# Norm steps that run as fill, queued behind the weight splits in a down projection

## The chip, the cores and the metric

The kernel runs on one core of a Trainium2 chip, in one launch. The metric is the device time of one execution in microseconds; the median of the runs counts. A core has TensorE (PE, matrix products), VectorE (DVE), ScalarE (ACT), GpSimd (POOL) and SyncE (SP). Each engine takes its instructions in a fixed order, and an instruction that waits holds what stands behind it on its engine. SP, POOL and ACT also issue DMAs from their queues.

## The reference

Two layers of a diffusion backbone over 1024 latent tokens and 256 context tokens, 1024 channels wide. What matters here is the end of layer 0, and the first norm of layer 1:

```python
def swiglu(u, w_gate, w_up, w_down):
    return (jax.nn.silu(u @ w_gate) * (u @ w_up)) @ w_down

def rms_norm(x, g):
    y = x32 * lax.rsqrt(jnp.mean(x32 * x32, axis=-1, keepdims=True) + RMS_EPS)
    return (y * g.astype(jnp.float32)).astype(x.dtype)
...
        h_lat = h_lat + g2 * swiglu(modulate(rms_norm(h_lat, norm2_g[i]), sh2, sc2), ...)
        if not last:
            h_ctx = h_ctx + cg1 * y_ctx
            h_ctx = h_ctx + cg2 * swiglu(modulate(rms_norm(h_ctx, norm2_g[i]), csh2, csc2), ...)
# next layer:
        u_lat = modulate(rms_norm(h_lat, norm1_g[i]), sh1, sc1)
```

## The kernel before, in words

Channels lie on the 128 partitions, eight blocks deep; tokens lie along the row. They come in pieces: latent half 0 and latent half 1 (512 tokens each, `pc` 0 and 1) and the context (256 tokens, `pc` 2).

Every product is exact to nearly float32 by a split: an operand x becomes `hi`, a rounded copy, and `lo = x - hi`, and the product is the sum of three, hi·hi, hi·lo and lo·hi. `split` makes them: a cast on ACT (L287), then a subtraction on DVE (L289). It notes both instructions in `self.last_hi` and `self.last_lo`. In the context part the weight's halves are called `wh` and `wl`.

`down` (from L1424) is the last product of the feed-forward part. For the latent tokens it runs seven passes of 11 operand pairs each, a fast scheme of seven products in place of eight; each operand (1024 wide) is loaded by SP, split and used by 12 matmuls of 512 columns (L1445), into four accumulators. After a pass, `evict` (L1466) adds the accumulators to the residual on DVE, and `square` makes a square on ACT (L475) and adds it up on DVE (L480). In layer 0 the context part follows: a loop over 22 blocks `kb`. Each loads a weight of 128x1024 (`in_down`, 512 KB), splits it, and runs 24 matmuls of 256 columns (L1557). The staging tile of the weight is a `ws` (two buffers) for two of three blocks, and an `s` of the pool of twenty large tiles for each third (kb 2, 5, 8, 11 and so on); `wh` and `wl` have two buffers each. The context's hidden tile of a block (128x256) is loaded by POOL into one of 35 smaller tiles and split too.

The norm of layer 1 runs as fill in between: `after(pc)`, here `after2` (L1998), is a generator of six steps. The first two compute the scale of each token (`rms_begin`, `rms_end`), and each of the other four norms two channel blocks with `norm_block`: for a block one L522 on DVE (times scale), one L524 on ACT (rounded copy) and one L525 on DVE (the rest). The last reader of a residual tile frees its small buffer. The function `hook(i)` takes the next step; it is called at the start of each of the 11 operand pairs of a latent pass and of each `kb` of the context loop. Half 0's norm begins in the seventh latent pass, half 1's in the context loop. Steps are taken at i = 3 and 6, and in layer 0 at every i > 7.

The order on each engine is not written by hand. A scheduler makes it when the program is built, from the order of the program text, from dependencies and free buffers, and from its own estimate of when each instruction can run. `self.follow(ins)` gives it an edge: what is recorded inside the `with` stands behind `ins` on that instruction's engine. Other places use it already; `evict` stands behind `last_hi` and `last_lo`:

```python
with self.follow(self.last_hi if p < 6 else None), self.follow(self.last_lo if p < 6 else None):
    evict(acc, r, j, q, final)
```

Of the kernel before, what the change touches and what calls it, by code (L numbers as in the profile page):

```python
# [200 lines left out]
class Builder:  # L201
# [1222 lines left out]
    def down(self, l, bops, sops, hidc, hs, h, todo, after, keep):  # L1424
# [57 lines left out]
        done = iter(())  # L1482

        def hook(i):
            if i in (3, 6) or i > 7 and l == 0:
                next(done, None)

        def fetch(p, i):
            ak, bk = seq[p][:2]
# [6 lines left out]
        for p, (ak, bk, r, pc, final) in enumerate(seq):  # L1496
            acc = sets[p % 2]
            late = []
            for i in range(n2):
                hook(i)  # L1500
                if p == 0 and i == 6:
                    load_h(range(4), 1)
                if p == 1 and i in (1, 4, 7):
                    load_h(*((range(4), 0), (range(4, 8), 0), (range(4, 8), 1))[i // 3])
                ops = ready.pop(0) if ready else fetch(p, i)
                if p == 5 and i == n2 - 1:
                    mark = self.last_ld, self.last_hi, self.last_lo
                if p == 6 and i >= n2 - (4 if l else 3):
                    late.append((i, ops))
                else:  # L1510
                    with self.follow(end):
                        for j in range(4):
                            m = prods(acc, ops, j, 0, 512, p in (0, 1, 3) and i == 0, i == n2 - 1)
                    end = m
                if p < 5 and i % 2 or p == 5 and i < 2:
                    next(todo, None)
# [14 lines left out]
            if p == 5:  # L1531
                done = after(0)
        if l == 0:
            for _ in done:
                pass
            done = after(1)
            acc = [self.PP() for _ in range(4)]
            for kb in range(NFB):
                hook(kb)
                if kb in (4, 8, 12, 16):  # L1540
                    load_h((kb // 2 - 2, kb // 2 - 1), 2)
                t = self.S2(F32R)
                f = t[:, 256:].bitcast(F32)
                with self.follow(self.last_ldr):
                    self.ldr(f, hidc[kb // 2][:, kb % 2])
                self.split(f, t[:, :256], t[:, 256:])
                f = self.pw.tile([P, 1024], F32, tag="ws", name=self.nm("ws")) if kb % 3 < 2 else self.S4()
                wh, wl = self.pair1()
                with self.follow(mark[0]), self.follow(mark[1]), self.follow(mark[2]):
                    self.ld(f.rearrange("p (r k) -> p r k", r=2), w[kb].rearrange("r p k -> p r k"))  # L1550
                    self.split(f, wh, wl)
                for nb in range(KB):

                    o = acc[nb // 2][:, nb % 2 * 256:nb % 2 * 256 + 256]
                    with self.follow(end):
                        for k, (x, c) in enumerate(((wh, 0), (wh, 256), (wl, 0))):
                            m = nc.tensor.matmul(o, x[:, nb * P:(nb + 1) * P], t[:, c:c + 256],  # L1557
                                                 start=kb == 0 and k == 0 and nb % 2 == 0,
                                                 stop=kb == NFB - 1 and k == 2, skip_group_check=True)
                    end = m.ins  # L1560
# [640 lines left out]
```

## Time and profile before

| what | value |
|---|---|
| median of 3 runs | 3024.45 us (3024.08 to 3025.89) |
| profiled execution | 3021.79 us, its span 3020.0 us |
| PE busy | 2894.4 us (96%) |
| PE weight loads (PEld) busy | 2414.6 us (80%) |
| DVE busy | 2079.7 us (69%) |
| ACT busy | 1363.0 us (45%) |
| POOL busy | 478.9 us (16%) |
| DMA | 558.26 MB, mean 185 GB/s |

The profile is of one execution, and its times count from the start of the span. A row of the timeline gives start, duration, engine, line of the kernel, operation, the tiles written and read with their shapes, how many instructions were merged into the row, and in brackets how long the engine had been idle before it and what ended that. SPq is the queue on which SP issues DMAs. Adjacent rows of one engine overlap a little, since the end of one instruction runs beside the start of the next.

### The profile page before, as it was taken

Reading aid. Unit: us, or ns where it says so; the run is one execution under the profiler, and the core shown is the slowest. Engines: PE = TensorE matmul, PEld = TensorE weight load, DVE = VectorE, ACT = ScalarE, POOL = GpSimd, SP = SyncE. Lnnn points to the kernel's source line nnn. Section 1 sums busy time; section 2 is a strip of 40 time slices with the busy share of each in tenths; the row PEclk is TensorE's granted clock in tenths of the full one; section 3 lists DMA queues with packets and bytes.
Section 4 is the critical chain, followed back from the end, with each engine's and each line's share of the span. In section 5 each row is a group of like instructions: output and inputs, shape, how many; then the busy total and the mean of one; then the engine's idle time right before and its main releaser. Section 6 shows DMA issues by size and latency. Waiting matters only on the chain. (4 is left out here: it accounts for less than half of the span.)

```text
span 3020.0 us, 45776 instructions
## 1 busy us (share of the span) xinstructions
PE 2894.4 (96%) x16320; PEld 2414.6 (80%) x16320; DVE 2079.7 (69%) x3988; ACT 1363.0 (45%) x2549; POOL 478.9 (16%) x785
## 2 busy tenths in 40 slices
PE   7899999999999999999999999999899999999997
PEld 2678888888899788788888888878777788888886
DVE  5677786675677777876777437777677977665454
ACT  3453325453455333333445337777675533333442
POOL 1112013452100111112020000110111022112000
PEclk9899999999999999999999999999999999999998
DMA  8764545456555554659884344444555266435663
GB/s 279 247 222 168 178 146 172 122 181 230 189 183 196 174 185 170 213 186 324 318 291 155 126 129 118 129 139 124 177 184 203 89 235 216 175 113 184 212 194 119
DMA packets 263486, 558.26 MB, mean 185 GB/s; under 512 B 33878, under 2 KB 85784, under 8 KB 263258
## 3 DMA queue, kind: packets, MB, share of 16 engines
q1 hardware_dynamic: 205050, 372.84, 37.8%
q0 software_dynamic: 55904, 178.30, 16.5%
q10 hardware_dynamic: 2304, 4.20, 0.4%
q8 instruction: 128, 2.10, 0.3%
q14 instruction: 100, 0.82, 0.1%
HBM read 418.63 MB, written 119.80 MB: 178 GB/s over the span
## 5 line engine op out<-in xcount | busy, mean ns | idle before, releaser
L1274 PE MATMUL ps<-s,s 128*128 128x512 f32 x2028 | 505.9, 391 | 12.8 <-ACT g L1279 4.6
L1274 PEld LDWEIGHTS ps<-s,s 128*128 128x128 f32 x2028 | 380.9, 188 | 97.2 <-ACT g L1279 7.1
L283 PE MATMUL ps<-s,wh 128*128 128x256 f32 (+1 forms) x1768 | 393.4, 328 | 2.3 <-DVE s L720 1.2
L283 PEld LDWEIGHTS ps<-s,wh 128*128 128x128 f32 x1768 | 292.7, 189 | 38.1 <-ACT wh L287 2.5
L283 PE MATMUL pq<-s,wh 128*128 128x512 f32 (+1 forms) x984 | 299.4, 383 | 0.6 <-DVE s L1658 0.6
L287 ACT CAST wh<-ws 128x1024 fp32r<-128x1024 f32 (+1 forms) x139 | 142.4, 1024 | 334.7 <-PE ps L283 158.4
L1445 PE MATMUL ps<-s,s 128*128 128x512 f32 (+1 forms) x1000 | 258.4, 383 | 4.5 <-DVE s L289 4.4
L289 DVE TENSOR_TENSOR wl<-ws,wh 128x1024 fp32r<-128x1024 f32 (+1 forms) x139 | 165.3, 1190 | 136.0 <-ACT wh L287 134.2
L283 PE MATMUL ps<-s,wl 128*128 128x256 f32 (+1 forms) x884 | 255.8, 326 | 1.2 <-DVE wl L289 1.2
L287 ACT CAST s<-s 128x1024 fp32r<-128x1024 f32 (+2 forms) x184 | 168.2, 940 | 187.9 <-DMA s<-d 169.6
L283 PE MATMUL ps<-s,s 128*128 128x64 f16 (+3 forms) x2663 | 217.0, 233 | 24.3 <-DVE st L1743 10.3
L287 ACT CAST s<-t 128x512 fp32r<-128x512 f32 (+2 forms) x250 | 139.7, 579 | 182.2 <-DVE t L1253 68.4
L289 DVE TENSOR_TENSOR s<-s,s 128x1024 fp32r<-128x1024 f32 (+2 forms) x162 | 186.8, 1184 | 46.9 <-ACT s L287 46.4
L1445 PEld LDWEIGHTS ps<-s,s 128*128 128x128 f32 x1000 | 184.4, 188 | 42.9 <-DVE s L289 6.7
L289 DVE TENSOR_TENSOR s<-t,s 128x512 fp32r<-128x512 f32 (+2 forms) x250 | 166.9, 680 | 57.8 <-ACT s L287 31.2
L283 PEld LDWEIGHTS pq<-s,wh 128*128 128x128 f32 x984 | 177.7, 190 | 34.2 <-DVE s L1658 2.1
L1274 PE MATMUL ps<-s,wh 128*128 128x512 f32 x608 | 193.3, 395 | 0.3 <-DVE g L1367 0.3
L283 PE MATMUL ps<-s,mat 128*128 128x512 f32 x684 | 178.5, 408 | 4.9 <-ACT s L287 4.0
L283 PE MATMUL pq<-s,wl 128*128 128x512 f32 (+1 forms) x492 | 182.1, 380 | 0.0
L283 PEld LDWEIGHTS ps<-s,wl 128*128 128x128 f32 x884 | 162.6, 188 | 18.4 <-DVE wl L289 1.9
L283 PEld LDWEIGHTS ps<-s,mat 128*128 128x128 f32 x684 | 132.3, 196 | 39.8 <-ACT s L287 6.2
L1445 PE MATMUL ps<-s 128*128 128x512 f32 (+1 forms) x500 | 149.4, 385 | 0.0
(381 smaller groups left out, 5621.8 us busy)
## 6 DMA issues: line engine op xcount, KB each, us to landing
s<-d SPq DMA_DIRECT2D x282, 256.0 KB, 3.6
s<-in_down SPq DMA_DIRECT2D x150, 256.0 KB, 4.0
d<-s POOLq DMA_DIRECT2D x137, 256.0 KB, 3.6
d<-tk POOLq DMA_DIRECT2D x98, 256.0 KB, 3.6
s<-in_ada_w POOLq DMA_DIRECT2D x48, 512.0 KB, 4.7
g<-in_bias SPq DMA_DIRECT2D x128, 192.0 KB, 2.8
ws<-in_up SPq DMA_DIRECT2D x44, 512.0 KB, 3.4
d<-g POOLq DMA_DIRECT2D x87, 256.0 KB, 3.1
```

The costliest lines, as they stand in the source:

```text
L283: self.nc.tensor.matmul(o, l, r, start=st, stop=sp)
L287: self.last_hi = nc.scalar.copy(hi, src).ins
L289: self.last_lo = eng.tensor_tensor(lo, src, hi.bitcast(F32), SUB).ins
L1274: nc.tensor.matmul(ps, x[:, sl], y, start=first and j == 0 and x is wh and y is xh, stop=j == 3 and x is wl, skip_group_check=True)
L1445: m = nc.tensor.matmul(acc[j][:, c0:c1], x[:, sl], y[:, xs], start=first and k == 0, stop=last and k == 2, skip_group_check=True)
```

## The change

The step that `hook` takes is recorded under two edges when i > 7: on ACT behind the last cast of a split (`last_hi`), on DVE behind its subtraction (`last_lo`). Steps at i = 3 and 6 get none. When `hook(i)` is called, the last split is that of the operand or block before i. Only layer 0 takes steps at i > 7; they are those of half 0 at i = 8 to 10 of the seventh latent pass, and those of half 1 at kb 8 to 11 of the context loop. The number of instructions, their shapes and the tiles stay the same.

```diff
         def hook(i):
             if i in (3, 6) or i > 7 and l == 0:
-                next(done, None)
+                with self.follow(self.last_hi if i > 7 else None), self.follow(self.last_lo if i > 7 else None):
+                    next(done, None)
```

## The prediction

> **What bounds the kernel now.** I read the page first, for the busy shares; then, because the change touches one stage only, the timeline of that stage engine by engine, its windows, and its DMA queues. Times below are microseconds from the start of the span.
>
> ```profile
> span 3020.0 us, 45776 instructions
> PE 2894.4 (96%) x16320; PEld 2414.6 (80%) x16320; DVE 2079.7 (69%) x3988; ACT 1363.0 (45%) x2549; POOL 478.9 (16%) x785
> ```
>
> TensorE (PE) is busy for 96% of the span, so a change gains only where PE stands still, and costs wherever it makes PE stand still. PE's timeline, in the stage from the last latent pass of layer 0's down projection through the context part, has these rows (idle time and its releaser in brackets):
>
> ```profile
> 1585.91 2.11 PE L1445 MATMUL ps<-s,s 128*128 128x512 f32 x8 [1.59 <-DVE s L289]
> ...
> 1603.41 0.50 PE L1557 MATMUL ps<-s,wh 128*128 128x256 f32 x2
> ...
> 1623.34 0.39 PE L1557 MATMUL ps<-s,wh 128*128 128x256 f32 x2
> 1624.61 0.39 PE L1557 MATMUL ps<-s,wl 128*128 128x256 f32 x1 [0.87 <-DVE wl L289]
> ...
> 1629.71 0.39 PE L1557 MATMUL ps<-s,wl 128*128 128x256 f32 x1 [2.11 <-DVE wl L289]
> ```
>
> Three stalls, and each waits for the subtraction of a split (L289 on DVE, VectorE). The DVE timeline shows why:
>
> ```profile
> 1581.32 3.40 DVE L522 SCALAR_TENSOR_TENSOR t<-s,c,t 128x512 f32<-128x512 f32 x5
> 1584.64 2.35 DVE L289 TENSOR_TENSOR s<-s,s 128x1024 fp32r<-128x1024 f32 x2
> ...
> 1600.14 1.22 DVE L289 TENSOR_TENSOR s<-s,s 128x1024 fp32r<-128x1024 f32 x1
> 1601.28 1.41 DVE L525 SCALAR_TENSOR_TENSOR s<-t,c,s 128x512 fp32r<-128x512 f32 x2
> 1602.61 2.71 DVE L1466 SCALAR_TENSOR_TENSOR s<-ps,c,s 128x512 f32<-128x512 f32 x4
> ...
> 1619.36 3.39 DVE L522 SCALAR_TENSOR_TENSOR t<-s,c,t 128x512 f32<-128x512 f32 x5
> 1622.67 0.74 DVE L525 SCALAR_TENSOR_TENSOR s<-t,c,s 128x512 fp32r<-128x512 f32 x1
> 1623.33 1.22 DVE L289 TENSOR_TENSOR wl<-ws,wh 128x1024 fp32r<-128x1024 f32 x1
> ```
>
> Five norm steps (L522, 0.66 each from 3.40/5) run in one go ahead of a subtraction that PE needs. After the third stall comes a fourth loss, in the windows of one microsecond (columns: length; busy time of PE, PEld, DVE, ACT, POOL; PE clock; DMA share; GB/s):
>
> ```profile
> 1630.00:1631.00 1.00, 1.00 (x9) 1.00 (x9) 1.00 (x3) 0.64 (x1) 0.00 (x0) 0.76 1.04 375
> 1631.00:1632.00 1.00, 1.00 (x7) 1.00 (x7) 1.00 (x1) 0.08 (x1) 0.00 (x0) 0.50 1.17 328
> 1632.00:1633.00 1.00, 1.00 (x6) 1.00 (x6) 1.00 (x3) 0.00 (x0) 0.00 (x0) 0.50 0.89 344
> 1633.00:1634.00 1.00, 1.00 (x7) 1.00 (x6) 0.45 (x1) 0.02 (x1) 0.00 (x0) 0.53 0.75 242
> ```
>
> The granted clock is short by 0.24 + 0.50 + 0.50 + 0.47 = 1.71 us. So the most that this stage can give is 1.59 + 0.87 + 2.11 + 1.71 = 6.28 us, just over 0.2% of 3024.45 (6.05 us, about what a measurement of this kernel tells from no change).
>
> **The change part by part.** No instruction is added or removed. From hook i = 8 on, the norm steps (L522 and L525 on DVE, L524 on ACT, ScalarE) get an order edge behind the last split. I compared the order in which the two built kernels issue. The blocks of the context loop are named kb; their loads stand on SP's queue like this (ws and s are the two kinds of staging buffer):
>
> ```
> before: ws kb9, s kb8, ws kb10, s kb11, s kb14, s kb17, s kb20, ws kb12, ws kb13
> after:  ws kb9, ws kb10, s kb8, ws kb12, ws kb13, s kb11, s kb14, s kb17, s kb20
> ```
>
> On ACT, in the last pass, the six small casts (128x256) of context hidden tiles, which stood together, now stand one by one between the norm steps and the last big casts (1024 wide). POOL's queue is unchanged, but its loads wait for buffers that L522 releases.
>
> *The last pass.* The three big subtractions come first, so the stall of 1.59 goes. What is late next is a load:
>
> ```profile
> 1582.36 3.28 POOL L274 DMA_DIRECT2D s<-d x6 [43.93 <-DMA s<-in_down]
> 1592.89 1.20 POOL L274 DMA_DIRECT2D s<-d x2 [7.25 <-DVE t L522]
> ...
> s<-d POOLq DMA_DIRECT2D x8, 128.0 KB, 3.0
> ...
> 1581.18 2.00 ACT L287 CAST s<-s 128x1024 fp32r<-128x1024 f32 x2
> 1586.21 0.41 ACT L287 CAST s<-s 128x256 fp32r<-128x256 f32 x1 [3.04 <-DMA s<-d]
> ```
>
> POOL issues as L522s release buffers (the second row names it; the 43.93 of the first is a releaser long done, since the issue follows the first L522). Landing takes 3.0, and ACT waits for it. Now the L522s come later, in pairs, and a big cast that PE needs stands behind each small cast. In steps: big casts at 1.0 each from 1581.18; three subtractions, 1.15 apart (2.35 for two), to 1585.6; L522 twice to 1586.9; L525 twice behind their L524, 1588.5; next subtraction behind its cast, 1589.8; third L522, 1590.6. POOL issues then, the tile lands at 1594.0, small cast 0.33, big cast to 1595.3, subtraction to 1596.5, fifth L522 to 1597.2. Again a load: 1600.3, small cast, last big cast to 1601.5, last subtraction 1601.6 to 1602.8 against 1600.14 + 1.22 = 1601.4 before. Then DVE has two small subtractions (0.34 each) and two L525 (1.41), and the evictions L1466 begin at 1605.0 instead of 1602.61. PE's first context matmul at 1603.41 stands behind the first eviction (1602.61 + 0.74 = 1603.35), so it slips by **2.4**, the gained 1.59 already used up. If the loads landed at once, the pass would end about 1 us earlier than now; if every small cast waited out a full landing, about 3 later than I have it: -1 to +5.
>
> *The context loop*, on the times of before. A block takes PE 2.72 (1623.34 to 1626.06, without stall). Its cast (1.05) starts when the block two earlier has ended, since wh and wl have two buffers each. DVE now stands idle before kb 7's subtraction instead of running norm steps, so that one ends at 1623.0 rather than 1623.33 + 1.22 = 1624.55, and the 0.87 goes. The loads decide what is late next:
>
> ```profile
> 1610.42 9.42 SPq L268 DMA_DIRECT2D ws<-in_down  x3
> 1619.93 0.42 SPq L268 DMA_DIRECT2D s<-in_down  x1
> 1624.58 0.37 SPq L268 DMA_DIRECT2D ws<-in_down  x1
> 1625.04 5.02 SPq L268 DMA_DIRECT2D s<-in_down  x4
> ...
> ws<-in_down SPq DMA_DIRECT2D x9, 512.0 KB, 3.9
> s<-in_down SPq DMA_DIRECT2D x7, 512.0 KB, 5.0
> ...
> 1624.41 1.05 ACT L287 CAST wh<-s 128x1024 fp32r<-128x1024 f32 x1
> ```
>
> ws has two buffers, so kb 10's load waits for kb 7's subtraction: 1624.58 is 0.03 behind 1624.55. Before, kb 8's load was already out at 1619.93, and its cast ran at 1624.41. Now it stands behind kb 10's: kb 10 at 1623.1, kb 8 at 1623.6 (0.46 apart, as 1624.58 to 1625.04). Landing takes between 3.9 and 5.0; I take 4.4, as 1619.93 to 1624.41 bounds it at 4.5. So: tile 1628.0, cast to 1629.05, subtraction to 1630.3. PE is free at 1626.06: it waits 2.9 for the cast and, two matmuls on, 1.0 for the subtraction: **3.9**. kb 8 ends at 1632.8; kb 9 is in time (two L522 and its subtraction by 1632.7). For kb 10 four norm steps (2.6) and the subtraction (1.15) go into 2.72 of PE time: **0.7** of stall, and kb 10 ends at 1638.9. kb 11's load stands behind kb 13's, which waits for kb 10's subtraction (1636.5): out at 1637.05, landed 1641.45, cast 1642.5, subtraction 1643.7. PE waits 3.6 and 1.0: **4.6**. In all 9.2 against 0.87 + 2.11 = 2.98: **+6.2**. With landings of 3.9 it is +5.2, with 5.0 +7.4.
>
> *The clock.* The rows show half a clock for about 3.4 us after PE had been idle 2.98 in some 6 us, and no idle time as long as the coming ones. I take one such stretch after kb 8 and one after kb 11, 1.71 each, against one before: **+1.7**; bounds: none at all (-1.7) and two more stretches (+5.1). The Trainium skill, "TensorE: Matmul & The Clock Gate", HAM oscillation, warns only of PE-idle gaps over about 3.4 us: by that rule only kb 11's stall slows the clock, and the sum would be 1.7 smaller. The row speaks against it, since 2.11 in one piece was enough here.
>
> *Later work.* In layer 2 some neighbours swap places (splits against L1159 and L2030 near 2320). The view of PE's waits between 2318 and 2330 is empty, so I cost this at nothing, within 1 either way; PE's own backlog covers it. The norm's result is needed only by the projections after the loop, and these stay behind it.
>
> Sum: 2.4 + 6.2 + 1.7 = 10.3. The profiled execution took 3021.79 (its span and 1.79 around it) and would take 3032.1; the median of the runs is 2.66 above it, so the forecast on that scale is 3024.45 + 10.3 = 3034.7.
>
> **The rivals.**
> *The stalls go and nothing replaces them*: faster. All three rows name a subtraction behind norm steps, and the edge takes just these out of its way. It gives 3024.45 - 6.28 = 3018.2. It decides if kb 8's and kb 11's loads are not held, that is if a ws buffer is free when SP reaches the load; the 1624.58 row speaks against. Chance 0.06.
> *VectorE's own work decides, the loads do not*: no change to be told. From kb 7's subtraction to kb 11's DVE has 5 x 1.15 + 16 x 0.66 = 16.3 without a gap, from 1621.85 to 1638.2, where PE wants the last by 1623.34 + 4 x 2.72 + 0.2 = 1634.4: 3.8 of stall. Against 2.98 + 1.71, and with 2.4 from the last pass, that is +1.5: 3026.0. It needs loads that land within 1 us of issue, or a staging slot freed early. Chance 0.14.
> *The clock by the page's rule*: one slow stretch, as before, 8.6 in all and 3033.0. Chance 0.15; it changes no sign.
> *More slow stretches* (two more, after the last pass's idle 3 us and split windows): 10.3 + 3.4 = 13.7 and 3038.2. Chance 0.12.
> That the edge does nothing is excluded: the built order has moved on DVE, ACT and SP.
>
> **How the numbers follow.** Forecast 0.53, the rivals as given. The likeliest case by itself spans 3030 to 3038 (landings 3.9 to 5.0, the last pass 1 less or 2 more). The range 3025 to 3041 takes in both clock cases, the last pass at its upper bound and the upper half of the VectorE case; what is left out is the gain and the extremes of several bounds together. Slower by over 0.2% (above 3030.5): the forecast, both clock cases, less a little of each: 0.78. Within: 0.15. Faster: 0.07.
>
> **What would show it.** In the profile of the changed kernel: no idle row of 1.59 behind five L522; small casts on ACT that wait for POOL's loads in the last pass; kb 8's load on SP issued after kb 7's subtraction, and kb 11's after kb 10's; PE idle by some 3 before L1557 twice, released by the cast (ACT wh L287) and not by DVE; clock rows of 0.50 behind them. It is wrong if PE's idle time between 1580 and 1650 is under 5, or if the cast of kb 8 does not wait for its load.

## The result and the profile after

| what | before | after |
|---|---|---|
| median of 10 runs each, side by side | 3026.84 us (3023.28 to 3029.64) | 3037.02 us (3030.13 to 3052.25) |
| ratio | 1 | 1.0038 [1.0022, 1.0054] |
| profiled execution | 3021.79 us | 3052.25 us |

The change makes the kernel slower, by 10.2 us between the medians (6.7 to 16.3 by the interval of the ratio); the forecast was 10.3. The profiled execution of after is the longest of its ten, 30.5 above that of before, and half of this is not the change: the stage below begins 14.3 later in its span (1597.52 against 1583.25), with the same work ahead of it, in the same order on PE. So only the stage itself is compared here, matmul by matmul.

"The stage" runs from the first matmul of one operand pair of layer 0's last latent pass (the pair whose stall of 1.59 is quoted in the prediction) to the first matmul of context block kb 13. Its length is counted from the timeline rows of these matmuls: 61.7 us before, 73.1 after, **+11.3**. Of this the last pass, up to the start of kb 4, has +2.8, the blocks kb 4 to 6 have nothing, and kb 7 to 12 have +8.5.

The page of after, its span and engines:

```profile
span 3050.3 us, 45773 instructions
PE 2908.6 (95%) x16320; PEld 2423.9 (79%) x16320; DVE 2078.1 (68%) x3988; ACT 1364.5 (45%) x2549; POOL 478.5 (16%) x785
```

DVE, ACT and POOL do the work of before. What PE waited for in the stage, before and then after (engine, line, releaser: us in all, times, longest):

```profile
PE ps L1557 <- DVE wl L289: 3.0, 2, 2.1
PE ps L1445 <- DVE s L289: 1.6, 1, 1.6
```

```profile
PE ps L1558 <- ACT wh L287: 6.9, 2, 4.2
PE ps L1445 <- ACT s L287: 3.0, 2, 2.6
PE ps L1558 <- DVE wl L289: 1.2, 2, 0.8
```

(L1558 is L1557 of before.) The waits for subtractions have shrunk from 4.6 to 1.2, as the edge wants; waits for casts, of which there were none, have come in their place, 9.9 in all. PE's timeline of after has them one by one:

```profile
1610.43 1.20 PE L1445 MATMUL ps<-s 128*128 128x512 f32 x4 [0.46 <-ACT s L287]
...
1616.36 1.56 PE L1445 MATMUL ps<-s 128*128 128x512 f32 x4 [2.56 <-ACT s L287]
...
1646.07 0.50 PE L1558 MATMUL ps<-s,wh 128*128 128x256 f32 x2 [2.73 <-ACT wh L287]
...
1647.33 0.39 PE L1558 MATMUL ps<-s,wl 128*128 128x256 f32 x1 [0.76 <-DVE wl L289]
...
1661.35 0.80 PE L1558 MATMUL ps<-s,wh 128*128 128x256 f32 x2 [4.18 <-ACT wh L287]
...
1662.61 0.58 PE L1558 MATMUL ps<-s,wl 128*128 128x256 f32 x1 [0.46 <-DVE wl L289]
```

The first two are in the last pass, the next two in kb 8, the last two in kb 11. Why the casts are late is in ACT's timeline:

```profile
1607.49 0.41 ACT L287 CAST s<-s 128x256 fp32r<-128x256 f32 x1 [4.41 <-DMA s<-d]
...
1614.95 1.97 ACT L287 CAST s<-s 128x256 fp32r<-128x256 f32 x4 [1.18 <-DMA s<-d]
...
1644.97 1.04 ACT L287 CAST wh<-s 128x1024 fp32r<-128x1024 f32 x1 [2.75 <-DMA s<-in_down]
...
1660.26 1.04 ACT L287 CAST wh<-s 128x1024 fp32r<-128x1024 f32 x1 [3.51 <-DMA s<-in_down]
```

Each waits for a load. The first two are the small context tiles of the last pass; the second row merges four casts, one of them the big one that PE waits for until 1616.36. The other two are the weights of kb 8 and kb 11. POOL's row and SP's queue show when these loads were issued, and DVE what SP had waited for:

```profile
1612.59 1.86 POOL L274 DMA_DIRECT2D s<-d  x3 [5.87 <-DVE t L522]
```

```profile
1627.37 13.16 SPq L268 DMA_DIRECT2D ws<-in_down  x4
1640.62 0.42 SPq L268 DMA_DIRECT2D s<-in_down  x1
1649.77 4.63 SPq L268 DMA_DIRECT2D ws<-in_down  x2
1654.48 3.62 SPq L268 DMA_DIRECT2D s<-in_down  x4
```

```profile
1638.91 1.22 DVE L289 TENSOR_TENSOR wl<-ws,wh 128x1024 fp32r<-128x1024 f32 x1 [2.35 <-ACT wh L287]
...
1652.77 1.23 DVE L289 TENSOR_TENSOR wl<-ws,wh 128x1024 fp32r<-128x1024 f32 x1 [0.38 <-ACT wh L287]
```

kb 7's subtraction ends at 1640.13, kb 10's load goes out, and only then, at 1640.62, kb 8's, which the cast of 1644.97 wants. kb 10's subtraction ends at 1654.00, kb 13's load goes out, and then, at 1654.48, the first of four `s` loads, kb 11's. In before, kb 8's load stood ahead of the one that waits.

Last the clock. In windows over the whole stage (length; busy time of PE, PEld, DVE, ACT, POOL; PE clock; DMA share; GB/s), before and after:

```profile
1575.00:1645.00 70.00, 65.25 (x433) 58.27 (x432) 53.51 (x70) 40.30 (x59) 4.25 (x8) 0.98 0.54 180
```

```profile
1594.00:1672.00 78.00, 66.80 (x422) 59.87 (x421) 51.98 (x67) 37.09 (x53) 4.27 (x8) 0.91 0.44 144
...
1618.00:1620.00 2.00, 2.00 (x6) 1.54 (x6) 2.00 (x4) 0.16 (x1) 0.00 (x0) 0.50 0.00 0
...
1648.00:1650.00 2.00, 2.00 (x12) 2.00 (x11) 2.00 (x3) 1.36 (x2) 0.00 (x0) 0.50 0.00 0
...
1662.00:1664.00 2.00, 1.54 (x7) 1.39 (x7) 1.69 (x2) 0.25 (x1) 0.00 (x0) 0.50 0.43 164
1664.00:1666.00 2.00, 2.00 (x12) 2.00 (x11) 0.00 (x0) 0.00 (x0) 0.00 (x0) 0.50 0.50 176
```

Half a clock follows the stall in the pass, the one of kb 8 and, twice as long, the one of kb 11: 13.7 us in all by the clock's records, 3.4 before.

### The profile page after: what moved, and what is told of

Same layout as the page of the kernel before. It is cut to its first block, busy times and chain, and to the rows that moved or that the text cites. A ratio compares the mean times of both kernels' runs of the same rounds, so it can differ in the third digit from the quotient of the medians.

```text
span 3050.3 us, 45773 instructions
## 1 busy us (share of the span) xinstructions
PE 2908.6 (95%) x16320; PEld 2423.9 (79%) x16320; DVE 2078.1 (68%) x3988; ACT 1364.5 (45%) x2549; POOL 478.5 (16%) x785
## 3 DMA queue, kind: packets, MB, share of 16 engines
q0 software_dynamic: 55904, 178.30, 16.2%
## 4 chain that ended last, share of the span: by engine, by line
PE 49%; issue 15%; DMA 6%; DVE 6%; ACT 2%; POOL 2%; SPq 0%; POOLq 0%; DVEq 0%; ACTq 0%
PE ps L283 15%; PE ps L1274 12%; PE pq L283 9%; PE ps L1445 5%; PE pq L1274 3%; PE ps L1558 2%; PE pq L1445 1%; DMA g<-in_bias 1%; PE ps L1756 1%; POOL d L274 1%; DMA s<-in_down 1%; DMA s<-d 1%; DMA ws<-in_up 1%; DVE s L289 1%; DMA ws<-in_gate 0%
```

## The experiments

Theory: the edge takes the norm steps out of the subtractions' way, but loads are held by it: in the loop on SP's queue, in the pass through POOL's loads, which wait for L522. Rivals: VectorE's own norm work decides and the loads don't matter; or the clock carries most of it. The tables give the median of the runs, the ratio to the kernel before on the same chip with its interval, and the stage's length in the profiled execution.

### Where the cost sits: the loop alone, the pass alone

A flag `ctx` is set where the context part begins; each kernel keeps the edge on one side of it.

```diff
-with self.follow(self.last_hi if i > 7 else None), ...
+with self.follow(self.last_hi if i > 7 and ctx else None), ...        # loop alone
+with self.follow(self.last_hi if i > 7 and not ctx else None), ...    # pass alone
```

(`last_lo` in the same way.) Expected of the loop alone:

> The edges only in the context loop (blocks 8 to 11), none in the last latent pass. Theory (loads held on SP): the pass stays as before, with PE's stall of about 1.6 behind five norm steps; in the loop PE waits about 3.5 to 4 at block 8 and 4.5 at block 11, released by the cast. Time +8 us against before (+6.2 of stalls, +1.7 of slow clock), 2.4 less than the full change. Rival (VectorE's own work decides): 3.8 us of stall spread over blocks 8 to 11 and released by the subtraction, time within 1 us of before.

Expected of the pass alone:

> The edges only in the last latent pass, none in the context loop. Theory (small casts wait for POOL's loads): SP's loads go out in the order of before, the loop keeps its stalls of 0.9 and 2.1 and one slow stretch of the clock; in the pass the stall of 1.6 goes but PE waits about 3 for the last big cast and 1 for the first eviction: +2.4 us against before. Rival (the edge only clears the way in the pass): 1.6 us faster than before.

| kernel | median (kernel before: 3019.78) | ratio | stage |
|---|---|---|---|
| loop alone | 3034.97 | 1.0047 [1.0035, 1.0059] | 71.3 |
| pass alone | 3022.41 | 1.0011 [1.0000, 1.0021] | 62.9 |

PE's waits in the stage, loop alone, then pass alone (L1560 is L1557 of before):

```profile
PE ps L1560 <- ACT wh L287: 7.4, 2, 4.6
PE ps L1445 <- DVE s L289: 1.6, 1, 1.6
PE ps L1560 <- DVE wl L289: 1.5, 2, 0.8
```

```profile
PE ps L1445 <- ACT s L287: 3.3, 2, 2.5
PE ps L1560 <- DVE wl L289: 3.0, 2, 2.1
PE ps L1560 <- DVE s L1466: 0.6, 1, 0.6
```

The two halves nearly add up: the edge in the loop makes the 7.4 for casts (6.9 in after), the edge in the pass turns 1.6 into 3.3 (3.0 in after). PE's 0.6 for the evictions (L1466) in the pass alone has no counterpart in after, where PE, at half a clock, comes to them later. The loop carries most of the cost, 9.6 us of the stage against 1.2; the 1.2 is small because the pass alone has no slow stretch, where before has one in the loop, worth 1.7. By the totals the loop alone is 15.2 us slower than before where 8 were expected, and it isn't below the whole change (1.0047 against 1.0038, intervals that overlap), where 2.4 less was expected. The pass, up to kb 4, takes 33.9 with the edge (after, pass alone, and the next kernel) and 30.2 to 31.1 in the six kernels that leave it as before or only move ACT's steps.

### The loads given back their place

After, with the loads of kb 8 and later kept in the order in which the text names them, and before with the same, as a control.

```diff
-with self.follow(mark[0]), self.follow(mark[1]), self.follow(mark[2]):
+with self.follow(mark[0]), self.follow(self.last_ld if kb > 7 else None):
     self.ld(f.rearrange("p (r k) -> p r k", r=2), w[kb].rearrange("r p k -> p r k"))
+with self.follow(mark[1]), self.follow(mark[2]):
     self.split(f, wh, wl)
```

Expected of after with this order:

> The full change, and SP issues the context weights of blocks 8 to 21 in the order of the blocks, so that no load stands behind one that waits for a later subtraction. Theory: PE's waits for the casts of blocks 8 and 11 go, some 1 to 4 us of waits for subtractions are left in the loop, and the pass costs +2.4 as in the full change: 1 to 4 us slower than before, about 7 faster than the full change. Rival (VectorE's own work or the clock decides, not the loads): as slow as the full change, +10.

Expected of before with it:

> The kernel before with the same order of loads on SP, as a control. Theory: its loads were in time already, so within 1 us of before, with the stalls of 1.6, 0.9 and 2.1 where they were. Rival (the order of the loads is worth something by itself): 2 us or more faster than before, with less idle time before blocks 7 and 8.

| kernel | median (kernel before: 3019.78) | ratio | stage |
|---|---|---|---|
| after, loads in order | 3023.53 | 1.0014 [1.0003, 1.0025] | 63.7 |
| before, loads in order | 3023.43 | 1.0007 [0.9998, 1.0015] | 59.2 |

SP's queue and PE's waits in after with the loads in order (L1559 is L1557):

```profile
1613.89 0.42 SPq L268 DMA_DIRECT2D s<-in_down  x1
1619.93 3.94 SPq L268 DMA_DIRECT2D ws<-in_down  x2
1623.96 0.42 SPq L268 DMA_DIRECT2D s<-in_down  x1
```

```profile
PE ps L1445 <- ACT s L287: 2.8, 2, 2.5
PE ps L1559 <- DVE wl L289: 2.2, 3, 0.9
PE ps L1559 <- ACT wh L287: 0.9, 1, 0.9
```

This is the decisive pair. The edge on the engines is the same as in after; only the loads stand elsewhere, and the waits for casts in the loop fall from 6.9 to 0.9, the stage by 9.4. Of the 9.4, 5.1 is the clock: after has 10.2 us at half a clock in the loop, this kernel none. The three kernels whose loads are held (after, loop alone, and "spread only" below) have 10.2 to 13.7 there, the seven others none or 3.4. By the totals it is 1.0014 of before, where the whole change is 1.0038. kb 8's load goes out at 1613.89, some 11 us ahead of its cast. What is left in the loop is 2.2 + 0.9 = 3.1 for norm work that is too dense (the cast of the 0.9 stands behind an L524 on ACT), and the wait for casts in the pass stays, 2.8. In before the order of loads changes nothing that the total can tell, and the waits stay 3.0 and 1.6: there, no load was late.

### The ACT edge alone

```diff
+with self.follow(self.last_hi if i > 7 else None):
     next(done, None)
```

> Only the edge on ScalarE behind the last cast (pass and loop), none on VectorE. The norm's VectorE steps come first and ScalarE's steps wait for them, so the edge on ScalarE moves little: time within 2 us of before, with the stall of 1.6 in the pass and two of 1 to 2 in the loop. Rival (ScalarE's edge carries the cost of the change): 5 us or more slower than before.

3022.38 against 3021.80, ratio 1.0003 [0.9993, 1.0013], stage 60.2: no cost. PE waits 1.6 in the pass and 1.6 in the loop, where 2 to 4 were expected. (The DVE edge alone was not run: its built program has the same order on every engine as the whole change.) So it is the edge on DVE from which the scheduler's new order of the loads comes.

### The norm steps spread out

Two kernels have the edge in the loop alone and let `after2` yield after each channel block of half 1, so that a step brings one L522, one L524 and one L525 and not two of each. One of them also has the loads in order.

```diff
-                if b % 2:
+                if b % 2 or pc == 1:
                     yield
```

Expected with the loads in order:

> Edges in the context loop only, one channel block of the norm per loop block (8 to 15) in place of two (8 to 11), and SP's loads of blocks 8 to 21 in the order of the blocks. Theory: per loop block VectorE has 2 x 0.66 + 1.15 = 2.5 us of work against PE's 2.72, and no load is held, so the stalls of 0.9 and 2.1 and the slow stretch of the loop go and nothing replaces them: from the first matmul of the last pass's third operand pair to block 13 about 57 to 58 us against 61.7 before, time 2 to 4 us faster than before. Rival (any edge makes PE wait, or the loads matter little): the loop keeps 3 us or more of stalls, time as before or slower.

Expected without:

> The same without the order of the loads: the scheduler again puts block 8's load behind block 10's and block 11's behind block 13's. Theory: PE waits about 3 us for the cast of block 8 and 2 to 4 for that of block 11 although VectorE has little to do: 4 to 8 us slower than before. Rival (VectorE's bunched norm steps make the stalls): as fast as with the loads in order, 2 to 4 us faster than before.

| kernel | median (kernel before: 3021.80) | ratio | stage |
|---|---|---|---|
| spread, loads in order | 3021.68 | 1.0000 [0.9988, 1.0012] | 57.1 |
| spread only | 3039.31 | 1.0064 [1.0048, 1.0081] | 71.3 |

PE's waits in the stage, with the loads in order (L1561 is L1557), then without (L1560):

```profile
PE ps L1445 <- DVE s L289: 1.6, 1, 1.6
PE ps L1561 <- DVE wl L289: 1.4, 3, 0.6
```

```profile
PE ps L1560 <- ACT wh L287: 10.9, 3, 5.5
PE ps L1560 <- DVE wl L289: 2.0, 3, 0.8
PE ps L1445 <- DVE s L289: 1.6, 1, 1.6
```

With the load order of the scheduler, thinner norm work doesn't help: the waits for casts grow to 10.9, since kb 8's, kb 11's and kb 14's loads are all held (that last wait, 2.7 + 0.8, lies behind the end of the stage). With the loads in order, the loop's waits fall from the 3.0 of before to 1.4 (the last 0.6 of them in kb 14, behind the end of the stage), and the stage falls by 4.6 to 57.1, as expected; 1.7 of the 4.6 is the slow clock of before that doesn't come here. The total shows none of it, where 2 to 4 were expected: its interval is ±0.12%, 3.6 us. In the profiled execution the part behind the stage took 7.6 longer than in before; its waits there sum to 51.7 against 49.2, and it has 9.1 more at half a clock, which costs 4.5. Whether these belong to the kernel or to the execution isn't settled; the same sum of waits is 48.7 to 52.6 in four other kernels here.

### The small casts out of the pass

The pass alone, with the splits of the last context tiles (kb > 14) set behind the pass's last split:

```diff
+            hi6, lo6 = self.last_hi, self.last_lo      # where the context part begins
 ...
+                with self.follow(hi6 if kb > 14 else None), self.follow(lo6 if kb > 14 else None):
                     self.split(f, t[:, :256], t[:, 256:])
```

> Edges only in the last latent pass, and the splits of the context hidden tiles of blocks 15 to 21 queued behind the last split of the pass, so that no small cast that waits for POOL's load stands ahead of a big one. Theory: PE's wait of about 3 us for the last big cast goes; the pass to block 4 takes about 31 us, as before (31.0), in place of about 34 in the kernel with the edges in the pass alone. Rival (VectorE's norm steps themselves delay the last split): it stays at 33 to 34.

3023.64 against 3021.80, ratio 1.0015 [1.0003, 1.0027], stage 63.6. PE's waits in the stage (L1562 is L1557):

```profile
PE ps L1562 <- DVE wl L289: 3.0, 2, 2.1
PE ps L1562 <- DVE s L1466: 1.9, 2, 1.0
PE ps L1445 <- DVE s L289: 0.2, 1, 0.2
```

The pass's 3.3 for casts are gone, so they were due to the small casts that wait for POOL's loads. With them goes the whole delay up to the end of the pass: the last big subtraction ends 16.2 after the start of the stage, against 18.1 before and 20.4 in the pass alone, and the first context matmul behind the pass starts at 19.3, against 20.2 and 23.1. So the rival falls: the norm steps by themselves don't delay the last split. That the pass up to kb 4 takes 32.9 all the same, not the 31 expected, comes from what lies behind that matmul. DVE, then PE (the stage starts at 1581.13):

```profile
1599.61 0.74 DVE L1466 SCALAR_TENSOR_TENSOR s<-ps,c,s 128x512 f32<-128x512 f32 x1
1600.27 1.40 DVE L525 SCALAR_TENSOR_TENSOR s<-t,c,s 128x512 fp32r<-128x512 f32 x2
1601.60 2.06 DVE L1466 SCALAR_TENSOR_TENSOR s<-ps,c,s 128x512 f32<-128x512 f32 x3
```

```profile
1600.41 0.51 PE L1562 MATMUL ps<-s,wh 128*128 128x256 f32 x2 [0.89 <-DVE s L1466]
...
1602.39 0.79 PE L1562 MATMUL ps<-s,wh 128*128 128x256 f32 x2 [1.02 <-DVE s L1466]
```

Two norm steps (L525) now stand between the first eviction and the others; PE waits 1.0 for the second, and 3.4 us at half a clock follow (0.59 and 0.55 in the windows of two microseconds from 1602 to 1606), which cost 1.7. Most of what was won at the last split is lost again here, and the total shows no gain over the pass alone (1.0015 against 1.0011).

## Why the prediction was right

Sign, size and the mechanism of both places held; the terms are off in both directions by less than the range allowed. That forecast and medians agree to 0.1 is luck: the interval of the measured difference is 6.7 to 16.3, and the terms as measured in the profiled stage sum to 11.3, with errors that partly cancel.

- **The stall of 1.59 and what takes its place.** No row of 1.59 behind five L522 is left, and a load is late next, twice, as forecast. The steps were +2.4 for the pass; it is +2.8 against the profile of before and 2.8 to 3.7 against all kernels that leave the pass alone. PE's waits for casts (0.46 and 2.56) are not the end of it: the evictions on DVE, which stand behind the last split, begin 22.0 after the start of the stage, against 19.4 before, 2.6 later where the working had 2.4. The pass takes 33.9 both with half a clock in it (after) and without (pass alone): in after PE comes to the context matmuls at 1620.84, 0.6 behind the end of the first eviction, so the half clock costs 0.6 here at most. (The matmul at 1603.41 that the working calls PE's first context matmul is the first behind the pass; twelve of kb 0 had run from 1593.29.)
- **kb 8.** 2.73 + 0.76 = 3.49 against 3.9. The load took 4.35 from issue to cast, near the 4.4. The subtraction cost 0.76, not 1.0, since the two matmuls ahead of it took 0.50, twice what I had.
- **kb 10.** 0.7 forecast, no wait in after. I had PE run on at full clock; at half a clock behind kb 8's stall it loses 1.7 and reaches kb 10 at 1654.29, when kb 10's subtraction has ended, at 1654.00. With the loads in order, when PE doesn't lose that time, such waits do appear: 2.2 for subtractions, in three places.
- **kb 11.** 4.18 + 0.46 = 4.64 against 4.6, but by two errors that cancel. The landing was taken at 4.4 and took 5.7 (from 1654.48 to 0.1 ahead of the cast at 1660.26). Why isn't shown. Four `s` loads go out in that row behind kb 13's, but such a row stands in before too (1625.04), and there the first landed in 4.4. In after a packet of instructions (q8, 16 KB) is under way beside them, in before none; in "spread only", beside such a packet, two loads with none behind them took 6.5 and 7.3. The DMA view between 1650 and 1670 gives (the queue's packets, MB and share; then count, KB, median us to landing)

```profile
q8 instruction: 1, 0.02, 0.6%
...
ws<-in_down SPq DMA_DIRECT2D x4, 512.0 KB, 4.1
s<-in_down SPq DMA_DIRECT2D x4, 512.0 KB, 6.1
```

  In the other direction, kb 11's load went out 2.7 ahead of the end of kb 10, where I had 1.85, and the subtraction cost 0.46, not 1.0.
- **The loop in all.** Waits 8.1 against 3.0 before, +5.1 where the steps gave +6.2.
- **The clock.** Two stretches of 1.71 against one was the estimate, +1.7. Measured are 3.4 us at half a clock after kb 8 and 6.8 after kb 11, which cost 1.7 and 3.4, against 1.7 before: +3.4, the rest of the loop's +8.5 behind the +5.1 of waits. The estimate was half of what came, and the surplus makes good what the waits fell short of. A third stretch, in the pass, costs 0.6 at most by the first point.
- **VectorE's own work decides**, the rival with 0.14: with the loads in order, the loop's waits were 3.1, near the 3.8 that it had. As a second limit it is right; as the one that decides it falls, since it decides only when the loads are in time, and that they were not was the whole of the loop's loss.
- **The clock by the page's rule.** The Trainium skill, "TensorE: Matmul & The Clock Gate", HAM oscillation, warns of PE-idle gaps over about 3.4 us; here 0.50 stood behind gaps of 2.56 and of 2.73, so the trace doesn't bear out that shorter gaps are safe.

Left open: the totals scatter by more than the stage explains. "Spread only" is 0.64% slower, 19 us, with 9.5 in the stage and some 3.5 of the new wait in kb 14; from the first matmul to the stage it is 1570 to 1591 us, and from its end to the last matmul 1357 to 1371, in ten profiled executions whose work there is the same but for the order of a few instructions behind the stage (and for kb 14's wait). The execution with the longest first part (after) has the most time at half a clock there, 48 against 27 to 38 in the others; what makes an execution so isn't shown.

## What to carry to other kernels

An order edge on a compute engine is an edge on the DMA queues as well, if a scheduler lays them out by its own estimates: before costing what the engine gains, list each queue's order before and after, and look for a load that now stands behind one that waits for a buffer. An edge that moves fill later should be made together with an edge that keeps the loads in order of use, and the fill cut to what fits beside one block. Fill also frees buffers, so whoever loads into them is moved along with it.

## What the runs showed that was not expected

Half a clock doesn't follow from the length of the idle time alone. The same waits, 0.88 and 2.11 within 6 us, were followed by a slow stretch in before and by none in two other kernels; 2.47 of idle in the pass alone was followed by none either, where 2.56 in after was, and two waits of 0.89 and 1.02 in the last experiment were. The windows over the stage of before with the loads in order, and of the pass alone:

```profile
1585.00:1650.00 65.00, 60.40 (x451) 56.53 (x450) 49.77 (x65) 36.39 (x51) 2.62 (x5) 1.00 0.45 154
```

```profile
1575.00:1645.00 70.00, 63.02 (x451) 56.99 (x449) 52.65 (x67) 37.41 (x52) 4.27 (x8) 1.00 0.46 157
```

And a slow stretch in these ten stages lasts 3.4 or 6.8 us, never a length between. Since of two executions with the same waits one can have a stretch that the other lacks, 1.7 to 3.4 us of a difference between two single profiles may be this alone.
